# Chunked softmax attention on one core: where the softmax sum is divided out, and what runs ahead of the norm statistics

## The chip, the cores and the metric

One core of a Trainium2 chip runs the whole program in one launch. The metric is device time in microseconds (us), lower is better. The kernel before takes 3090.66 us, the median of three runs (3089.91 to 3095.58). Engines are named as in the profile: PE is TensorE (matrix products), PEld its weight loads, DVE is VectorE, ACT is ScalarE, POOL is GpSimd, SP is SyncE, which here only issues DMAs.

## The reference

A trunk of two layers over 1024 positions of width 1024, all in float32. Layer 0 holds two recurrent head groups, layer 1 the attention that is changed here; each layer ends in an MLP and a gated embedding. The attention, cut to what matters:

```python
def chunk_band_attention(h, w_qkv, q_g, k_g, rel_bias):       # h = rmsnorm(x, norm_mix_g[1])
    qkv = (h @ w_qkv).reshape(bsz, seq, 3, C_HEADS, C_HEAD_DIM)      # 16 heads of 64
    q = rmsnorm(qkv[:, :, 0], q_g) * (C_HEAD_DIM ** -0.5)
    k = rmsnorm(qkv[:, :, 1], k_g)
    v = qkv[:, :, 2]
    ...
    def one_chunk(c):                                         # 64 queries, 576 keys
        s = jnp.einsum('bqhd,bkhd->bhqk', q_c, k_b).astype(jnp.float32) + bias
        s = jnp.where(valid, s, -jnp.inf)
        prob = jax.nn.softmax(s, -1).astype(v.dtype)
        return jnp.einsum('bhqk,bkhd->bqhd', prob, v_b)
```

The softmax is exp(s - max) divided by its sum over the keys. The division can be done on the exponentials (a row of them has one query) or on the result of the product with v.

## The kernel before

**Numbers.** A float32 product is made from three products of a split type: each operand is rounded to float32r (hi) on ACT, and DVE computes the rest (lo). Hi times hi, hi times lo and lo times hi are added in PSUM. So each activation that is split costs one ACT and one DVE instruction (split_scaled, L349 to L353).

**The stages.** Layer 0 runs until about 880 us, its MLP and gate (tail) until 1680 us, the attention of layer 1 from there to about 2320 us, and then its tail. PE is given one order of work for the whole program.

**Order.** `run` drives several generators ("lanes") against a clock of its own (`self.now`, moved on by each matmul): a lane that yields the name of a stretch in the table LAT comes back when that many microseconds have gone by on this clock, and another lane is let in meanwhile. So LAT sets how much other PE work is placed between two stretches of one lane, and `attn_block1` is the time between a block's exponentials and its transposes. Beyond that, the order on each engine's queue is fixed when the program is built: instructions are placed when their operands are expected, earlier code first. On the chip each queue runs in this order; an instruction that waits holds up what stands behind it.

**Attention.** There are 16 steps (8 pairs of heads pr, times two halves hf of 512 queries). Four lanes run (layer1_in):

- `attn_ins` runs `attn_in` for each step: for 128 positions at a time (index i = 4 hf + e) 24 matmuls of 128x384 (q, k and v of a pair) into one PSUM bank (L1854 to L1856). The input is not yet divided by its root mean square. This factor belongs to a position, so it is applied when the bank is read: an ACT copy for q and k (L1861), an ACT copy (L1865) and a DVE rest (L1866) for v, all with `rscol[:, i]`. At the first projection of all, `row_stats` computes `rscol`: a matmul for each 128 positions of the squares (accs, added up by POOL at L1627, in two halves) with a column of ones, 16 in the trace, one DVE scaling (L375), and an inverse root in ten small DVE steps (rsqrt_small). The projections and the statistics take their banks from a pool of two (`self.bank`, profile name dps).
- `attn_norms` brings q and k to feature rows and splits them (F and Ql).
- Two lanes of `attn_block` share the 64 blocks (step, head h, block blk of 256 queries). A block has two query tiles m of 128. For each: scores of the near keys (bank sn) and the far keys (bank sf), bias and maximum on DVE (L1957, L1965, L1966), exponentials with their sum on ACT (L1967 far, L1970 near), sum (L1972), reciprocal (L1973), and a scaling of up to 640 exponentials by it on ACT (L1974). After `attn_block1`: transposes on PE into banks pt (L192), split into ptile (L349, L350), product with v into the bank po, whose rows are features and whose columns are queries. Behind the second block of a head, ACT copies one half of po (otmp, L2015), and DVE adds the other half to it, giving y (L2016, 64 rows of a head by 512 queries). After both heads y is stored by an SP DMA (L2022); the last y is split in place.

PSUM has eight banks here: two dps, two sn, one sf, one o (po), two pt. On the SP queue of the stage are weight loads (L1823, three of 512 KB for a pair, through two buffers wraw; splits L1824 and L1825), bias tables (toep, L1841) and stores of y.

Of the kernel before, what the change touches and what calls it, by code (L numbers as in the profile page):

```python
# [8 lines left out]
F32 = mybir.dt.float32  # L9
F32R = mybir.dt.float32r  # L10
I32 = mybir.dt.int32
AF = mybir.ActivationFunctionType
ALU = mybir.AluOpType
# [4 lines left out]
P = 128  # L18
T = 1024
D = 1024  # L20
NK = D // P
HB = 512
# [61 lines left out]
    "gdn_back4": 1.83,  # L84
    "attn_norm0": 0.24,
    "attn_block0": 0.97,
    "attn_block1": 4.45,
    "attn_block2": 0.43,
    "attn_block3": 0.94,
    "qk": 11.25,  # L90
# [19 lines left out]
class Trunk:  # L110
# [252 lines left out]
            nc.scalar.activation(sq, src, AF.Square)  # L363
            nc.gpsimd.tensor_tensor(acc, acc, sq, op=ALU.add)

    def row_stats(self, accs, out, scale=1.0 / D, eps=1e-6):

        nc = self.nc
        nt = out.shape[-1]
        ps = self.stat_bank()  # L370
        for i in range(nt):
            self.mm(ps[:, i:i + 1], accs[i // 4][:, (i % 4) * P:(i % 4 + 1) * P], self.ones[:, 0:1],
                             start=True, stop=True)
        ms = self.sm.tile([P, NT], F32, tag="ms", name="ms")[:, 0:nt]
        nc.vector.tensor_scalar(ms, ps[:, 0:nt], scale, eps, op0=ALU.mult, op1=ALU.add)  # L375
        self.rsqrt_small(out, ms, [P, nt], "n")
# [1451 lines left out]
    def attn_in(self, pr, hf, l1, kv):  # L1828

        nc, a, psm = self.nc, self.a, self.psm  # L1830
        V, A, G = nc.vector, nc.scalar, nc.gpsimd
        wp = self.wp
        if hf == 0:
            raw = lambda: self.wr.tile([P, T], F32, tag="wraw", name="wraw")
            w = self.load_qkv(pr, raw) if pr else self.wq
            kv.clear()
            kv.update(w=w, toep=[], vs=[])
            for h in range(2):
                hd = 2 * pr + h
                t = l1.tile([P, 3 * P], F32, tag="toep", name="toep", bufs=3)  # L1840
                nc.sync.dma_start(out=t, in_=a["rb"][hd])  # L1841
                kv["toep"].append(t)
        wh, wl = kv["w"]
        qk = wp.tile([P, 4, 256], F32, tag="qk", name="qk")
        vs = l1.tile([P, 4, 2, P], F32R, tag="vs", name="vs", bufs=4)
        kv["vs"] = kv["vs"] + [vs]
        for e in range(4):
            i = 4 * hf + e
            ps = self.bank([P, 3, P])
            ts = slice(i * P, i * P + P)  # L1850
            for k in range(NK):
                ks = slice(k * P, k * P + P)
                xh, xl = self.xg[k][:, 0, ts], self.xg[k][:, 1, ts]
                self.mm(ps, xh, wh[:, :, ks], start=k == 0, stop=False)  # L1854
                self.mm(ps, xh, wl[:, :, ks], start=False, stop=False)
                self.mm(ps, xl, wh[:, :, ks], start=False, stop=k == NK - 1)  # L1856
                yield 0
            if pr == 0 and i == 0:
                self.row_stats(self.accs, self.rscol)
            rc = self.rscol[:, i:i + 1]  # L1860
            A.activation(qk[:, e, :], ps[:, 0:2, :].rearrange("p a c -> p (a c)"), AF.Copy, scale=rc)  # L1861
            v3 = ps[:, 2, :].rearrange("p (h d) -> p h d", h=2)
            vf = vs[:, e].rearrange("p h c -> p (h c)").rearrange("p (q d) -> p q d", d=64)
            hi = vf[:, 0:4:3, :]
            A.activation(hi, v3, AF.Copy, scale=rc)  # L1865
            V.scalar_tensor_tensor(vf[:, 1:3, :], v3, rc, hi.bitcast(F32), op0=ALU.mult, op1=ALU.subtract)  # L1866
            yield 0
        q4 = qk.rearrange("p i c -> p (i c)").rearrange("p (n d) -> p n d", d=64)
        ss = self.sm.tile([P, 16], F32, tag="ss1", name="ss1")
        nn = self.sm.tile([P, 16], F32, tag="nn1", name="nn1")  # L1870
        for e in range(2):
            sq = wp.tile([P, 8, 64], F32, tag="sq", name="sq", bufs=1)
            G.tensor_tensor(sq, q4[:, 8 * e:8 * e + 8], q4[:, 8 * e:8 * e + 8], op=ALU.mult)
            V.tensor_reduce(ss[:, 8 * e:8 * e + 8], sq, op=ALU.add, axis=AX.X)
        V.tensor_scalar(ss, ss, 1.0 / 64, 1e-6, op0=ALU.mult, op1=ALU.add)
        self.rsqrt_small(nn, ss, [P, 16], "q")
        V.tensor_tensor(q4, q4, nn.rearrange("p (n o) -> p n o", o=1).broadcast_to((P, 16, 64)), op=ALU.mult)
        return dict(kv, qk=qk)
# [28 lines left out]
    def attn_block(self, s, pr, hf, h, blk, l1, rbl):  # L1907

        nc, psm, sm = self.nc, self.psm, self.sm
        V, A, G = nc.vector, nc.scalar, nc.gpsimd  # L1910
        st = self.st[s]
        m0 = 4 * hf + 2 * blk
# [4 lines left out]
        hs = slice(64 * h, 64 * h + 64)  # L1917
        Q, Ql, K, vs, toep = st["Q"], st["Ql"], st["K"], st["vs"], st["toep"][h]

        def score(ps, m, j0, n):  # L1920
            qs = slice((m % 4) * P, (m % 4) * P + P)
            o = 0
            while o < n:
                j = j0 + o
                e = min(n - o, 4 - j % 4)
                ks = slice((j % 4) * P, (j % 4 + e) * P)
                k = K[j // 4]
                self.mm(ps[:, o * P:(o + e) * P], Q[:, h, qs], k[:, h, ks], start=True, stop=False)
                self.mm(ps[:, o * P:(o + e) * P], Ql[h][:, qs], k[:, h, ks], start=False, stop=True)
                o += e  # L1930
# [6 lines left out]
        place, bank, off = {}, 0, 0  # L1937
        for j, c0, c1 in segs:
            if off + c1 - c0 > HB:
                bank, off = bank + 1, 0  # L1940
# [3 lines left out]
        for j, (b, o, c0, c1) in place.items():  # L1944
            used[b] = max(used[b], o + c1 - c0)
        probs = []
        for m in (m0, m0 + 1):
            n0 = max(0, m - 2)
            nn = m - n0 + 1
            f0 = max(0, m - 4)  # L1950
            nf = n0 - f0
            pn = psm.tile([P, HB], F32, tag="sn", name="sn", bufs=2)
            score(pn[:, 0:nn * P], m, n0, nn)
            mx = sm.tile([P, 4], F32, tag="mx", name="mx", bufs=4)
            pb = self.wp.tile([P, 5 * P], F32, tag="pb", name="pb", bufs=4)
            S = pb[:, nf * P:(nf + nn) * P]
            V.tensor_tensor_reduce(S, pn[:, 0:nn * P], toep[:, (3 - nn) * P:], op0=ALU.add, op1=ALU.max,  # L1957
                                   scale=1.0, scalar=NEG, accum_out=mx[:, 0:1])
            l = sm.tile([P, 4], F32, tag="l", name="l", bufs=4)
            if nf:  # L1960
                pf = psm.tile([P, HB], F32, tag="sf", name="sf")
                score(pf[:, 0:nf * P], m, f0, nf)
                if m >= 4:
                    V.memset(pf[64:128, 0:64], NEG)
                V.reduce_max(mx[:, 1:2], pf[:, 0:nf * P], axis=AX.X)  # L1965
                V.tensor_scalar(mx[:, 2:3], mx[:, 0:1], mx[:, 1:2], -1.0, op0=ALU.max, op1=ALU.mult)  # L1966
                A.activation(pb[:, 0:nf * P], pf[:, 0:nf * P], AF.Exp, bias=mx[:, 2:3], accum_out=l[:, 1:2])  # L1967
            else:
                V.tensor_scalar(mx[:, 2:3], mx[:, 0:1], -1.0, None, op0=ALU.mult)
            A.activation(S, S, AF.Exp, bias=mx[:, 2:3], accum_out=l[:, 0:1])  # L1970
            if nf:
                V.tensor_tensor(l[:, 0:1], l[:, 0:1], l[:, 1:2], op=ALU.add)  # L1972
            V.reciprocal(l[:, 2:3], l[:, 0:1])  # L1973
            A.activation(pb[:, 0:(nf + nn) * P], pb[:, 0:(nf + nn) * P], AF.Copy, scale=l[:, 2:3])  # L1974
            probs.append((pb, f0))
            yield "attn_block0"
        yield "attn_block1"

        job = 4 * s + 2 * h + blk
# [6 lines left out]
        for b in range(bank + 1):  # L1986
            pt = psm.tile([P, HB], F32, tag="pt", name="pt", bufs=2)
            for j, (bb, o, c0, c1) in place.items():
                if bb != b:
                    continue  # L1990
                for e in range(2):
                    if c0 <= 128 * e < c1:
                        pb, f0 = probs[e]
# [8 lines left out]
        q = 0  # L2002
        for j, c0, c1 in segs:
            b, o, _, _ = place[j]
# [4 lines left out]
        if blk == 1:  # L2009
            if h == 0:  # L2010
                st["y"] = l1.tile([P, HB], F32, tag="y", name="y", bufs=1)
            y, po = st["y"], st["po", h]
            oth = slice(64 * (1 - h), 64 * (1 - h) + 64)
            tmp = l1.tile([P, HB], F32, tag="otmp", name="otmp", bufs=1)
            A.copy(tmp[hs], po[oth])  # L2015
            V.tensor_tensor(y[hs], po[hs], tmp[hs], op=ALU.add)  # L2016
            if h == 1:
                if s == 15:
                    yield ("ylast", 0)
                    self.split_scaled(self.ylast, y, None, slice(0, HB))  # L2020
                else:
                    nc.sync.dma_start(out=self.yd[pr][hf], in_=y)  # L2022
                self.dump("y1", y, (pr, slice(None), slice(hf * HB, hf * HB + HB)))
                self.mark(("at", s))
# [92 lines left out]
```

## Time and profile before

| what | before |
|---|---|
| median of three runs | 3090.66 us |
| the profiled execution | 3089.73 us |
| its span in the trace | 3088.0 us |
| mean granted PE clock | 0.978 of full speed |
| ACT busy in the whole span | 1510.7 us (49%) |
| POOL busy in the whole span | 544.9 us (18%) |

How to read the rows: a group has line, engine, operation, output <- inputs by the program's names, shapes, count | busy us, mean ns | idle time of the engine just before them <- what ended it. A timeline row has the start in us from the beginning of the span, the length in us, then engine, line and operation, in brackets the idle time before it and its releaser. A wait row has who waited <- for whom: us in total, times, longest. A window row has start:end, length, then the busy time of PE, PEld, DVE, ACT and POOL with their instruction counts, then the granted PE clock, the share of the DMA engines and GB/s. L177 and L192 are the helpers that issue every matmul and every transpose, so these go by the names of their tiles.

### The profile page before, as it was taken

Reading aid. Unit: us, or ns where it says so; the run is one execution under the profiler, and the core shown is the slowest. Engines: PE = TensorE matmul, PEld = TensorE weight load, DVE = VectorE, ACT = ScalarE, POOL = GpSimd, SP = SyncE. Lnnn points to the kernel's source line nnn. Section 1 sums busy time; section 2 is a strip of 40 time slices with the busy share of each in tenths; the row PEclk is TensorE's granted clock in tenths of the full one; section 3 lists DMA queues with packets and bytes.
Section 4 is the critical chain, followed back from the end, with each engine's and each line's share of the span. In section 5 each row is a group of like instructions: output and inputs, shape, how many; then the busy total and the mean of one; then the engine's idle time right before and its main releaser. Section 6 shows DMA issues by size and latency. Waiting matters only on the chain.

```text
span 3088.0 us, 47130 instructions
## 1 busy us (share of the span) xinstructions
PE 2979.5 (96%) x17288; PEld 2461.2 (80%) x17288; DVE 2232.1 (72%) x4518; ACT 1510.7 (49%) x2922; POOL 544.9 (18%) x978
## 2 busy tenths in 40 slices
PE   7999999999999999999999999989899999999999
PEld 5777778777777888888887988888788888888887
DVE  6656676657849788878867666766768888888762
ACT  4333443334427544444434577777756544544431
POOL 6533442443500000000015111100110000000002
PEclk9999999999999999999999999999999999999999
DMA  4211112211346434754424101100256444754432
GB/s 138 72 54 62 55 55 74 62 53 64 125 158 219 158 148 150 259 167 150 137 89 144 34 33 36 53 33 16 72 177 225 151 154 150 255 172 150 126 109 102
DMA packets 187639, 358.45 MB, mean 116 GB/s; under 512 B 45712, under 2 KB 47888, under 8 KB 187408
## 3 DMA queue, kind: packets, MB, share of 16 engines
q1 hardware_dynamic: 158608, 303.00, 29.6%
q10 hardware_dynamic: 28800, 52.44, 4.4%
q8 instruction: 136, 2.23, 0.3%
q14 instruction: 95, 0.78, 0.1%
HBM read 262.04 MB, written 93.32 MB: 115 GB/s over the span
## 4 chain that ended last, share of the span: by engine, by line
PE 79%; DVE 10%; ACT 4%; DMA 3%; POOL 2%; issue 2%; SPq 0%; DVEq 0%; POOLq 0%; ACTq 0%
PE dps L177 66%; PE ch L177 2%; PE pm L177 2%; PE iz L177 1%; PE po L177 1%; PE tp L177 1%; DVE ptile L350 1%; PE pt L192 1%; DVE pb L1957 1%; PE sn L177 1%; POOL subt L415 1%; PE py L177 1%; DMA wraw<-in_w_qkv 1%; ACT pb L1970 1%; POOL sub L417 1%
## 5 line engine op out<-in xcount | busy, mean ns | idle before, releaser
L177 PE MATMUL dps<-r,act 128*128 128x512 f32 x3528 | 829.4, 392 | 0.0
L177 PEld LDWEIGHTS dps<-r,act 128*128 128x128 f32 x3528 | 662.0, 188 | 145.8
L177 PE MATMUL dps<-xg,whi 128*128 128x512 f32 x1280 | 434.0, 419 | 14.9 <-ACT xg L352 7.4
L1614 POOL TENSOR_TENSOR pn<-pn,prs 128x512 f32<-128x512 f32 x32 | 47.1, 1474 | 1543.1 <-ACT prs L386 1447.7
L177 PE MATMUL dps<-wq,act 128*128 128x384 f32 x1536 | 305.7, 345 | 6.4 <-DVE vs L1866 3.1
L177 PEld LDWEIGHTS dps<-xg,whi 128*128 128x128 f32 x1280 | 233.9, 195 | 67.9 <-issue 8.0
L177 PEld LDWEIGHTS dps<-wq,act 128*128 128x128 f32 x1536 | 266.6, 191 | 10.5 <-DVE vs L1866 4.9
L177 PE MATMUL dps<-xg,wlo 128*128 128x512 f32 x640 | 258.8, 405 | 1.3 <-DVE wlo L304 1.3
L177 PE MATMUL dps<-late,act 128*128 128x512 f32 x960 | 229.2, 392 | 0.0
L177 PEld LDWEIGHTS dps<-late,act 128*128 128x128 f32 x960 | 180.3, 188 | 39.7
L1271 ACT CAST act<-act 128x512 fp32r<-128x512 f32 (+1 forms) x223 | 137.6, 649 | 131.6 <-PE dps L177 67.5
L1384 DVE TENSOR_TENSOR late<-late,dps 128x512 f32<-128x512 f32 x224 | 152.4, 684 | 52.2 <-PE dps L177 45.8
L1271 ACT CAST act<-late 128x512 fp32r<-128x512 f32 x210 | 124.2, 617 | 133.2 <-PE dps L177 90.4
L177 PE MATMUL dps<-act 128*128 128x512 f32 x672 | 165.0, 392 | 0.0
L1272 DVE TENSOR_TENSOR act<-act 128x512 fp32r<-128x512 f32 (+1 forms) x223 | 154.8, 721 | 6.0 <-ACT act L1271 5.8
L177 PEld LDWEIGHTS dps<-act 128*128 128x128 f32 x672 | 126.1, 188 | 28.7
L1272 DVE TENSOR_TENSOR act<-late,act 128x512 fp32r<-128x512 f32 x210 | 141.5, 688 | 8.9 <-ACT act L1271 7.0
L177 PEld LDWEIGHTS dps<-xg,wlo 128*128 128x128 f32 x640 | 124.4, 194 | 29.2 <-DVE wlo L304 1.8
L303 ACT CAST whi<-wraw 128x1024 fp32r<-128x1024 f32 x78 | 81.9, 1050 | 122.0 <-PE dps L177 82.4
L1522 DVE TENSOR_TENSOR xw<-xw,dps 128x512 f32<-128x512 f32 x174 | 118.0, 683 | 31.5 <-PE dps L177 31.5
L177 PE MATMUL dps<-xw,act 128*128 128x512 f32 x576 | 139.6, 392 | 0.0
L1389 ACT ACTIVATE late<-late 128x512 f32<-128x512 f32 x128 | 80.3, 630 | 119.4 <-DVE late L1384 113.5
(484 smaller groups left out, 5656.7 us busy)
## 6 DMA issues: line engine op xcount, KB each, us to landing
hb<-late ACTq DMA_DIRECT2D x168, 256.0 KB
act<-hb SPq DMA_DIRECT2D x138, 256.0 KB
late<-in_w SPq DMA_DIRECT2D x60, 512.0 KB
wraw<-in_w_in SPq DMA_DIRECT2D x56, 512.0 KB
act<-in_w SPq DMA_DIRECT2D x96, 256.0 KB
braw<-hb SPq DMA_DIRECT2D x72, 256.0 KB
wraw<-in_w_out SPq DMA_DIRECT2D x21, 512.0 KB
wraw<-in_w_qkv SPq DMA_DIRECT2D x21, 512.0 KB
```

What stands on the lines that cost most here:

```text
L177: return self.begin(self.nc.tensor.matmul(out, lhsT, rhs, start=start, stop=stop, skip_group_check=again))
L192: return self.begin(self.nc.tensor.transpose(out, in_, ident))
L303: nc.scalar.copy(hi, raw)
L350: nc.vector.tensor_tensor(dst[:, 1, sl], src, dst[:, 0, sl].bitcast(F32), op=ALU.subtract)
L415: E.tensor_tensor(o, X[:, 0:i, i:i + 1].broadcast_to((NP, i, n)), Bq[:, i:i + 1, i + 1:16].broadcast_to((NP, i, n)), op=ALU.mult)
L417: E.tensor_tensor(X[:, 0:i, i + 1:16], X[:, 0:i, i + 1:16], o, op=ALU.add)
L1271: A.copy(hi, s)
L1272: V.tensor_tensor(lo, s, hi.bitcast(F32), op=ALU.subtract)
L1384: V.tensor_tensor(r, t, u, op=ALU.add)
L1389: A.activation(t, t, AF.Relu)
L1522: V.tensor_tensor(x[n][:, hs[hf]], x[n][:, hs[hf]], ps, op=ALU.add)
L1614: G.tensor_tensor(pn, pn, prs[:, sl], op=ALU.mult)
```

## The change

Three things are edited.

1. **The projections of the first pair.** The first two (i = 0, 1) write to the score banks sn, which no block uses yet; the third takes a bank of the pool as before. Their three scalings are held back (`held`). The statistics are computed behind the third projection, in a bank pt, and then the three scalings are done. From the fourth on all is as before.
2. **The softmax sum.** The scaling of the exponentials is gone. The two reciprocals of a block are written to one tile rl (128 positions by 2). An SP DMA writes it to a row in DRAM (256 values of 4 bytes), one for each block. Behind the second block of a head a further SP DMA reads this row of 512 values back, to each of the 64 feature rows of the head (R). After the addition that gives y, DVE multiplies y by R.
3. **LAT.** `attn_block1` is 3.60 instead of 4.45.

```diff
-    "attn_block1": 4.45,
+    "attn_block1": 3.60,
...
-    def row_stats(self, accs, out, scale=1.0 / D, eps=1e-6):
+    def row_stats(self, accs, out, scale=1.0 / D, eps=1e-6, bank=None):
...
-        ps = self.stat_bank()
+        ps = bank if bank is not None else self.stat_bank()
...
+        def scale(i, e, ps):
+            rc = self.rscol[:, i:i + 1]
+            A.activation(qk[:, e, :], ps[:, 0:2, :].rearrange("p a c -> p (a c)"), AF.Copy, scale=rc)
+            v3 = ps[:, 2, :].rearrange("p (h d) -> p h d", h=2)
+            vf = vs[:, e].rearrange("p h c -> p (h c)").rearrange("p (q d) -> p q d", d=64)
+            hi = vf[:, 0:4:3, :]
+            A.activation(hi, v3, AF.Copy, scale=rc)
+            V.scalar_tensor_tensor(vf[:, 1:3, :], v3, rc, hi.bitcast(F32), op0=ALU.mult, op1=ALU.subtract)
+        held = []
         for e in range(4):
             i = 4 * hf + e
-            ps = self.bank([P, 3, P])
+            if pr == 0 and i < 2:
+                ps = psm.tile([P, HB], F32, tag="sn", name="dps", bufs=2)[:, 0:3 * P].rearrange("p (a c) -> p a c", a=3)
+            else:
+                ps = self.bank([P, 3, P])
...
-            if pr == 0 and i == 0:
-                self.row_stats(self.accs, self.rscol)
-            rc = self.rscol[:, i:i + 1]
...
+            held.append((i, e, ps))
+            if pr == 0 and i == 2:
+                self.row_stats(self.accs, self.rscol, bank=psm.tile([P, HB], F32, tag="pt", name="st", bufs=2))
+            if pr or i > 1:
+                for h in held:
+                    scale(*h)
+                held.clear()
...
+        rl = sm.tile([P, 2], F32, tag="rl", name="rl", bufs=4)
+        if blk == 0:
+            st["rd", h] = self.dr.tile([1, HB], F32, tag=f"rd{h}", name="rd", bufs=2)
+            if h == 0:
+                st["R"] = l1.tile([P, HB], F32, tag="R", name="R", bufs=2)
...
-            V.reciprocal(l[:, 2:3], l[:, 0:1])
-            A.activation(pb[:, 0:(nf + nn) * P], pb[:, 0:(nf + nn) * P], AF.Copy, scale=l[:, 2:3])
+            V.reciprocal(rl[:, m - m0:m - m0 + 1], l[:, 0:1])
...
+        rd = st["rd", h]
+        nc.sync.dma_start(out=rd[:, 256 * blk:256 * blk + 256].rearrange("o (e q) -> (o q) e", e=2), in_=rl)
+        if blk == 1:
+            nc.sync.dma_start(out=st["R"][hs], in_=rd.broadcast_to((64, HB)))
...
             V.tensor_tensor(y[hs], po[hs], tmp[hs], op=ALU.add)
+            V.tensor_tensor(y[hs], y[hs], st["R"][hs], op=ALU.mult)
```

More of the change, by code (lines that the diff above doesn't have):

```diff
@@ L1857, in attn_in @@
                 yield 0
-            if pr == 0 and i == 0:
-                self.row_stats(self.accs, self.rscol)
-            rc = self.rscol[:, i:i + 1]
[L1861 to L1866, printed above, removed]
+            held.append((i, e, ps))
[5 more added lines that the diff above has]
+                held.clear()
             yield 0
```

## The prediction

> **What bounds the kernel now.** I read the page first (busy shares), then the sums of the attention stage, then who TensorE waited for in it.
>
> ```profile
> span 3088.0 us, 47130 instructions
> PE 2979.5 (96%) x17288; PEld 2461.2 (80%) x17288; DVE 2232.1 (72%) x4518; ACT 1510.7 (49%) x2922; POOL 544.9 (18%) x978
> ...
> 1694.00:2320.00 626.00, 577.91 (x3517) 535.15 (x3518) 431.38 (x1361) 435.92 (x1011) 76.33 (x75) 0.97 0.17 59
> ...
> PE pt L192 <- ACT pb L1974: 8.4, 9, 1.8
> PE po L177 <- ACT ptile L349: 6.6, 14, 1.0
> PE po L177 <- DVE ptile L350: 6.1, 11, 1.4
> PE dps L177 <- POOL acc L1627: 4.8, 2, 4.1
> PE sf L177 <- ACT pb L1967: 4.0, 7, 1.5
> PE pt L192 <- DVE ptile L350: 4.0, 9, 0.9
> PE dps L177 <- DVE vs L1866: 3.1, 7, 0.8
> ```
>
> TensorE is busy 96% of the span, and the change touches none of its matmuls. Only its idle time can be won. In the attention stage (third row: window, length, then busy time of PE, weight loads, DVE, ACT, POOL, then granted clock) that is 626.00 - 577.91 = 48.1 us; nothing before 1680 us and after 2320 us is edited. The wait rows (total, times, longest) divide most of it: 8.4 us for the normalised exponentials (L1974), 6.6 and 4.0 us for other ScalarE results, 13.2 us for VectorE, and 4.8 us, before the window begins, for the squares of GpSimd. VectorE and ScalarE are both about 69% busy there, so work taken from one and given to the other is not free.
>
> **Part 1: three projections ahead of the statistics.** The rows below are PE, then ACT, then DVE in order of time, and last 2 us slices with the granted clock as third number from the end.
>
> ```profile
> 1685.81 0.45 PE L177 MATMUL dps<-wq,act 128*128 128x384 f32 x1 [0.32 <-DVE act L353]
> 1686.93 1.05 PE L177 MATMUL dps<-ones,acc 128*128 128x1 f32 x8 [0.68 <-POOL acc L1627]
> 1692.09 1.86 PE L177 MATMUL dps<-ones,acc 128*128 128x1 f32 x8 [4.11 <-POOL acc L1627]
> 1694.60 8.72 PE L177 MATMUL dps<-wq,act 128*128 128x384 f32 x33 [0.64 <-DVE ms L375]
> ...
> 1701.79 0.47 ACT L1861 ACTIVATE qk<-dps,rscol 128x256 f32<-128x256 f32 x1 [3.52 <-PE dps L177]
> 1705.95 0.47 ACT L1861 ACTIVATE qk<-dps,rscol 128x256 f32<-128x256 f32 x1 [3.42 <-PE dps L177]
> 1710.11 0.47 ACT L1861 ACTIVATE qk<-dps,rscol 128x256 f32<-128x256 f32 x1 [3.42 <-PE dps L177]
> ...
> 1702.16 0.36 ACT L1865 ACTIVATE vs<-dps,rscol 128x128 fp32r<-128x128 f32 x1
> 1702.56 0.35 DVE L1866 SCALAR_TENSOR_TENSOR vs<-dps,rscol,vs 128x128 fp32r<-128x128 f32 x1 [3.40 <-ACT vs L1865]
> ...
> 1694.38 0.16 DVE L375 TENSOR_SCALAR ms<-dps 128x8 f32<-128x8 f32 x1
> 1696.59 0.17 DVE L291 SCALAR_TENSOR_TENSOR rscol<-rsw,rscol 128x8 f32<-128x8 f32 x1
> ...
> 1688.00:1690.00 2.00, 0.00 (x0) 0.00 (x0) 0.91 (x2) 1.24 (x2) 1.79 (x2) 1.00 0.97 378
> 1692.00:1694.00 2.00, 1.86 (x8) 1.78 (x8) 1.88 (x2) 1.05 (x1) 1.35 (x5) 0.50 0.08 31
> 1698.00:1700.00 2.00, 2.00 (x8) 2.00 (x7) 1.16 (x2) 0.28 (x2) 0.00 (x0) 0.50 0.07 16
> 1700.00:1702.00 2.00, 2.00 (x12) 2.00 (x11) 0.00 (x0) 0.21 (x1) 0.00 (x0) 0.86 0.67 246
> ```
>
> Now the first projection ends at 1686.26, the statistics wait for the second half of the squares until 1692.09, and the second projection starts at 1694.60. In the idle time the granted clock falls to 0.50, so that projection takes 1701.79 - 1694.60 = 7.2 us, where the next ones take 4.16 (distance of the ACT rows). The fourth ends at 1710.1.
>
> Changed: projections two and three run on at once, 1686.3 + 2 x 4.16 = 1694.6. The squares are there at 1692.1, so the 16 statistics products (8 in 1.05 us at full clock) end at 1696.7 and the fourth projection at 1700.9: 9.2 us earlier. The fifth then needs the bank of the third. rscol is ready 2.4 us after the products (DVE rows), at 1699.1, and three held pairs of scalings at 0.83 each (0.47 and 0.36) end at 1701.6; with 0.35 for the DVE part (L1866) the bank is free near 1702, a stall of 1.2. Net **-8.0 us**. The queues of POOL and SP hold nothing of what is moved. Bounds: -9.2 without the stall, -4.8 if only the wait for the squares goes, 0 if the stage takes it back (a rival). I take -8.0 because the pieces are measured at this place, and TensorE has no wait there that hangs on something else.
>
> The Trainium skill (TensorE: Matmul & The Clock Gate, Part 1) puts the way back to full clock at one busy window of about 3.4 us. Here it took from 1692.09 to beyond 1700, longer. By the page the second projection would have lost about 1.7 us instead of 3.0, and the gain would be 6.7; the measured slices decide, so 8.0 stays.
>
> **Part 2: no scaling of the exponentials.**
>
> ```profile
> 1802.00 1.50 ACT L1974 ACTIVATE pb<-pb,l 128x640 f32<-128x640 f32 x3
> ...
> L1974 ACT ACTIVATE pb<-pb,l 128x640 f32<-128x640 f32 (+4 forms) x128 | 86.2, 694 | 18.4 <-DVE l L1973 15.5 <-DVE ss L1875 1.6 <-DVE rsw L290 0.9
> L2016 DVE TENSOR_TENSOR y<-po,otmp 64x512 f32<-64x512 f32 x32 | 22.0, 687 | 6.2 <-ACT otmp L2015 5.8
> ```
>
> 128 activations go, 86.2 us of ACT's 435.9, a fifth. The 9 waits of the transposes for them total 8.4, so 0.93 each; one activation takes 0.69 and a row of three (first line) holds the transposes 1.5 us after the last exponential. Taking away 0.69 of each 0.93 wins 9 x 0.69 = 6.2: **-6.2** (0 to -8.4). The other ACT waits (6.6 + 4.0) arise in the same queue; a fifth less load makes them a fifth smaller: **-2.1** (0 to -10.6). What is late next is the split on VectorE.
>
> attn_block1 falls from 4.45 to 3.60: the transposes are placed 0.85 us earlier in TensorE's order, about what the activation took (0.69). So I count it zero; if the exponentials aren't earlier by that much, each of the 9 waits keeps its length and the -6.2 is gone.
>
> **Part 3: the multiplication.** 32 tensor_tensor of 64x512 are added on VectorE. The addition of that shape (L2016) reads PSUM and takes 0.687; from SBUF I take the same: 22.0 us. Most of it falls in VectorE's 195 us of idle time. The stretch below (chain of waits, start, length) shows where it doesn't.
>
> ```profile
> 1857.83 1.15 DVE wq L1825
> ...
> 1859.00 3.73 DMA wraw<-in_w_qkv
> 1862.75 1.06 ACT wq L1824
> ...
> 1866.74 0.68 DVE y L2016
> ...
> 1859.00 6.42 SPq L1823 DMA_DIRECT2D wraw<-in_w_qkv  x3
> ...
> ACT wq L1824 <- DMA wraw<-in_w_qkv: 7.1, 5, 3.4
> ```
>
> At such a pair boundary, where the next weights are loaded and split, the addition lies on the chain, and the multiplication would too. Seven boundaries x 0.69 = **+4.8** (0 to 22.0, all 32).
>
> **Part 4: the way through DRAM.** No row before moves 4-byte runs. The nearest is a write and read back in layer 0, in timeline rows; under it the tightest pair of sum and use that I found, a second head of an odd half.
>
> ```profile
> 101.37 0.50 SPq L420 DMA_DIRECT2D z<-sub  x1
> 103.71 0.38 SPq L422 DMA_DIRECT2D Xp<-z  x1
> 106.08 0.40 ACT L442 ACTIVATE T<-Xp,half 128x128 f32<-128x128 f32 x1 [6.56 <-DMA Xp<-z]
> ...
> 1941.31 0.22 DVE L1973 RECIPROCAL l<-l 128x1 f32<-128x1 f32 x2
> 1948.93 0.69 DVE L2016 TENSOR_TENSOR y<-po,otmp 64x512 f32<-64x512 f32 x1
> ```
>
> Write to read is 2.34 us, read to use 2.37: 4.7 together. From the last reciprocal to the end of the addition there are 1949.62 - 1941.53 = 8.1 us, 7.4 without one scaling. So R is there, 2.7 us before it is wanted: 0, as an estimate with bounds 0 (hidden by transposes, splits and value products) and 13 (rival 4). In VectorE's queue the running maxima and splits stand behind a late multiplication, and TensorE behind these. On SP 64 writes and 32 reads are new, at the 0.38 to 0.50 of these rows 36 to 48 us of a stage of 626; what could stand behind them is the weight load at a boundary (rival 3). The last step's y is multiplied while TensorE has projection work: 0.
>
> **Sum:** -8.0 - 6.2 - 2.1 + 4.8 = -11.5 us. The profiled execution took 3089.73 (span 3088.0 and 1.73 around it); so 3078.2 for it, and its time is 0.93 below the median of 3090.66: forecast **3079**.
>
> **The rivals.**
> 1. Only the entry pays. For: the transposes are moved 0.85 earlier and wait as before. Against: ACT is relieved by a fifth. 3090.7 - 8.0 = 3082.7.
> 2. The relief pays in full: -8.0 - 8.4 - 10.6 and nothing for VectorE, 3090.7 - 27.0 = 3063.7. Against it: VectorE as busy as ACT.
> 3. Slower: R's read waits on SP for the landing of the write (2.34 us), once per head, and the third weight load of a pair stands behind it. The last row of part 3 shows ACT waiting for weights already (7.1 us in 5 times), so ACT and VectorE have no room there. Two heads per boundary, 2 x 2.34 x 6 weight loads within the stage = 28 us: 3079 + 28 = 3107. It decides against the change from 11.5 / 6 = 1.9 us a boundary on. Against: the new issues fill under a tenth of SP's time, so few need meet a weight load.
> 4. R late at VectorE: a weight load of 3.73 us ahead on the rings makes 4.7 into 8.4, 1.0 over the 7.4, at most at 8 second heads; with the queue behind each stalled by the same again, 8 x 1.6 = 13: 3092. The Trainium skill (DMA: Bandwidth & Descriptors, Latency and other measured facts) speaks for it, with HBM access rising to 2 us at high load; no run here shows that.
> 5. The change doesn't do what it says at the entry: the stage takes the 8.0 back at a later wait, 3090.7 - 3.5 = 3087.2.
>
> **How the numbers follow.** Forecast 0.46, rivals 0.13, 0.12, 0.15, 0.07, 0.07. 0.2% is about what a measurement here can tell from no change: 6.2 us, so the borders are 3084.5 and 3096.8. Faster: 0.44 of the forecast, 0.09 of rival 1, 0.12 = 0.65; within: 0.02 + 0.04 + 0.06 + 0.06 = 0.18; slower: 0.15 + 0.01 + 0.01 = 0.17. The forecast's own range is 3072 to 3084; with rival 2 whole and most of 4, 5 and part of 3 it becomes 3063 to 3100.
>
> **What would show it.** Right: three projections without a gap and a granted clock of 1.0 from 1686 to 1700; no ACT group of 86 us; TensorE idle in the attention stage down from 48 to about 44 us, and y's multiplication without a wait for R. Wrong: VectorE waiting for R or ACT longer for weights (rivals 3, 4), transposes that wait for L1970 as they did for L1974 (rival 1), or steps that keep their old distance from 2200 us although the first came 8 us earlier (rival 5).

## The result, and the profile after

The changed kernel takes 3191.51 us, the median of five runs (3189.26 to 3196.59), beside 3089.91 for the kernel before on the same chip: a ratio of 1.0329, 95% interval 1.0313 to 1.0344. It is slower by 3.3%, outside the prediction's range of 3063 to 3100. The profiled execution took 3196.59 us.

First the page of the changed kernel, and its attention stage in one window (columns as in the prediction's window rows):

```profile
span 3194.9 us, 47306 instructions
...
PE 3007.7 (94%) x17288; PEld 2491.6 (78%) x17288; DVE 2252.2 (70%) x4550; ACT 1430.2 (45%) x2794; POOL 541.4 (17%) x978
...
1696.00:2425.00 729.00, 596.78 (x3476) 553.92 (x3476) 454.64 (x1392) 354.50 (x882) 77.41 (x76) 0.90 0.26 56
```

The stage is 729 - 626 = 103 us longer, which is nearly all of the 106.9 us in the span. TensorE's idle time in it went from 48.1 to 132.2 us; its busy time rose by 18.9 us, with 41 products fewer in the window, while the mean granted clock fell from 0.97 to 0.90. The work moved as intended: ACT is busy for 354.5 us in place of 435.9, and the transposes wait 3.4 us for its exponentials where they waited 8.4 us for the scaling. What is new stands in the wait rows, SP's first:

```profile
SPq L1994 <- DMA rd<-rl: 254.8, 32, 10.3
...
DVE y L2035 <- DMA R<-rd: 52.3, 15, 8.6
DVE y L2034 <- DMA yd<-y: 46.0, 5, 12.2
PE po L177 <- DVE y L2034: 40.9, 7, 12.4
ACT wq L1777 <- DMA wraw<-in_w_out: 33.5, 8, 7.8
ACT wq L1824 <- DMA wraw<-in_w_qkv: 20.2, 8, 4.9
```

Line 1994 is the read of R. It waits on SP for the write `rd<-rl` to land, 254.8 / 32 = 8.0 us each time, where the prediction had 2.34. VectorE waits for R, and longer each time (5 waits, 46.0 us) for a transfer that the change doesn't touch: the store of y (`yd<-y`), which must have read y before y is written again. Weight loads are late too (L1777: 12.5 us before). One such place in the chain of waits (start, length, what), and TensorE in its last stretch:

```profile
1819.43 0.22 DVE rl L1988 x2
1819.80 0.48 DVE ptile L350
1820.28 8.14 DMA rd<-rl
1828.48 0.45 SPq L1994
1829.03 0.54 SPq L1992
1829.62 9.90 DMA yd<-y
1839.61 0.69 DVE y L2034
1840.35 2.08 PE po L177 x8
...
1829.60:1839.50 9.90, 0.00 (x0) 0.00 (x0) 0.00 (x0) 0.60 (x2) 0.00 (x0) 0.50 0.21 40
```

A write of 1 KB is issued at 1820.28, and SP sits 8.14 us until it has landed. Only then can the finished y be stored, behind the next write (L1992). That store takes 9.90 us, and VectorE and TensorE stand still meanwhile; the granted clock falls to 0.50. The engines of the DMA aren't full: their mean share is 0.21 there.

The entry, in timeline rows of PE, then DVE, then ACT:

```profile
1686.62 9.11 PE L177 MATMUL dps<-wq,act 128*128 128x384 f32 x51 [0.86 <-ACT act L352]
1695.56 1.84 PE L177 MATMUL st<-ones,acc 128*128 128x1 f32 x16
1697.27 4.41 PE L177 MATMUL dps<-wq,act 128*128 128x384 f32 x24
1705.42 6.86 PE L177 MATMUL dps<-wq,act 128*128 128x384 f32 x29 [3.75 <-DVE vs L1854]
...
1699.61 1.23 DVE L1825 TENSOR_TENSOR wq<-wraw,wq 128x1024 fp32r<-128x1024 f32 x1 [3.10 <-ACT wq L1824]
1700.75 0.16 DVE L375 TENSOR_SCALAR ms<-st 128x8 f32<-128x8 f32 x1
...
1698.52 1.05 ACT L1824 CAST wq<-wraw 128x1024 fp32r<-128x1024 f32 x1 [3.27 <-DMA wraw<-in_w_qkv]
```

Three projections run on without a gap, as predicted, and the fourth ends at 1701.7. But the fifth waits 3.75 us in place of 1.2: the statistics were ready at 1697.4, and `ms` (L375) stood behind the split of a weight (L1825) in VectorE's queue, which waited for ACT, and ACT for the load.

### The profile page after: what moved, and what is told of

Read it like the earlier page. It is cut to its first block, busy times and chain, and to the rows that moved or that the text cites. A ratio compares the mean times of both kernels' runs of the same rounds, so it can differ in the third digit from the quotient of the medians.

```text
span 3194.9 us, 47306 instructions
## 1 busy us (share of the span) xinstructions
PE 3007.7 (94%) x17288; PEld 2491.6 (78%) x17288; DVE 2252.2 (70%) x4550; ACT 1430.2 (45%) x2794; POOL 541.4 (17%) x978
## 4 chain that ended last, share of the span: by engine, by line
PE 73%; DMA 11%; DVE 8%; ACT 3%; POOL 2%; issue 2%; SPq 0%; DVEq 0%; POOLq 0%; ACTq 0%
PE dps L177 62%; DMA rd<-rl 4%; PE ch L177 2%; DMA yd<-y 1%; PE pm L177 1%; PE iz L177 1%; DMA wraw<-in_w_out 1%; PE po L177 1%; DMA R<-rd 1%; PE tp L177 1%; DMA wraw<-in_w_qkv 1%; POOL sub L417 1%; PE py L177 1%; PE sn L177 1%; POOL subt L415 1%
## 5 line engine op out<-in xcount | busy, mean ns | idle before, releaser
L177 PE MATMUL dps<-wq,act 128*128 128x384 f32 x1536 | 315.7, 355 | 10.4 <-DVE vs L1854 5.8
L177 PEld LDWEIGHTS dps<-wq,act 128*128 128x128 f32 x1536 | 278.6, 199 | 13.9 <-DVE vs L1854 6.9
L177 PE MATMUL po<-ptile,vs 128*128 128x256 f32 (+1 forms) x576 | 114.7, 313 | 63.7 <-DVE y L2034 40.9
L177 PEld LDWEIGHTS po<-ptile,vs 128*128 128x128 f32 x576 | 93.6, 215 | 72.7 <-DVE y L2034 31.6
```

The lines of the kernel that those rows point to most:

```text
L177: return self.begin(self.nc.tensor.matmul(out, lhsT, rhs, start=start, stop=stop, skip_group_check=again))
```

## The experiments

Four readings were open: the write's landing is long and all DMAs behind it come late; SP's wait blocks what stands behind it in its queue; R alone is late at VectorE; y's one buffer is the trouble. The table has the runs of the whole kernel; each ratio is to runs of the kernel before on the same chip. The last column is from one profile each: the span less the start of the first product of the attention with v, so that the entry is left out. It must be read with care where the entry itself differs: a shorter entry makes the first product earlier, and what the stage then takes back counts against that version.

| kernel | median us | ratio to before, 95% interval | first product to end, us |
|---|---|---|---|
| before | 3089.91 | 1 | 1341.4 |
| changed | 3191.51 | 1.0329 (1.0313 to 1.0344) | 1452.8 |
| e1 part 1 alone | 3086.54 | 0.998 (0.9968 to 0.9992) | 1336.9 |
| e2 no DMA | 3073.88 | 0.9934 (0.9916 to 0.9952) | 1324.1 |
| e3 DMAs, none awaited by VectorE | 3188.62 | 1.0298 (1.0275 to 1.0321) | 1446.0 |
| e4 runs of 8 bytes | 3091.17 | 0.9989 (0.9977 to 1.0) | 1341.4 |
| e5 two buffers for y | 3184.35 | 1.0289 (1.0263 to 1.0316) | 1428.9 |
| e6 = e4, reads from GpSimd | 3089.08 | 0.9982 (0.997 to 0.9995) | 1344.6 |
| e7 4 bytes, reads from GpSimd | 3207.99 | 1.0366 (1.0347 to 1.0384) | 1457.3 |
| e8 part 1 alone, four banks | 3081.02 | 0.9958 (0.9944 to 0.9972) | 1337.6 |
| e10 = e4, two y, four banks | 3083.57 | 0.9966 (0.9956 to 0.9976) | 1345.7 |
| e11 = e10, reads from GpSimd | 3088.89 | 0.9981 (0.9969 to 0.9994) | 1350.2 |
| e12 runs of 16 bytes | 3081.37 | 0.9967 (0.9957 to 0.9977) | 1329.5 |
| e13 = e12, four banks | 3084.75 | 0.9979 (0.9967 to 0.999) | 1344.1 |
| e14 = e13, two y | 3080.87 | 0.9967 (0.9958 to 0.9976) | 1341.8 |

**Which part costs.** e1 keeps the entry and puts the scaling of the exponentials back; e2 keeps all but the DMAs, and so leaves out the division.

```diff
-            V.reciprocal(rl[:, m - m0:m - m0 + 1], l[:, 0:1])
+            V.reciprocal(l[:, 2:3], l[:, 0:1])
+            A.activation(pb[:, 0:(nf + nn) * P], pb[:, 0:(nf + nn) * P], AF.Copy, scale=l[:, 2:3])   # e1
...
-        nc.sync.dma_start(out=rd[:, 256 * blk:256 * blk + 256].rearrange("o (e q) -> (o q) e", e=2), in_=rl)
-        if blk == 1:
-            nc.sync.dma_start(out=st["R"][hs], in_=rd.broadcast_to((64, HB)))                        # e1, e2
...
-            V.tensor_tensor(y[hs], y[hs], st["R"][hs], op=ALU.mult)
+            V.tensor_tensor(y[hs], y[hs], self.R1[hs], op=ALU.mult)      # e2, e3: a constant row
```

> Three projections ahead of the statistics, the exponentials scaled as before, attn_block1 at 4.45: part 1 alone. Before: 3090. Theory A (the loss is all in the way through DRAM): the fifth projection starts 4.6 us earlier relative to the end of the layer before, as in the changed kernel (1705.42 - 1.74 = 1703.7 against a fourth projection that ended at 1710.1 and a fifth that ended at 1714.3 before), and the stage keeps it: 3085 to 3086. Theory B (the stage takes it back at a later wait): 3089 to 3091. Theory C (part 1 shares in the loss): above 3095.

> The changed kernel without its 96 DMAs: y is multiplied by a constant tile, so the division by the softmax sum is left out. Theory A (the DMAs are the whole loss): what is left is part 1, the relieved ACT and the added multiplication, about -4.6 - 8.3 + 4.8 against before: 3078 to 3086. Theory C (the multiplication, attn_block1 or another order lose too): above 3095, and above 3150 if they are the larger part.

The entry alone gains 0.2%, 6 us. Without the 96 DMAs the changed kernel is 0.66% faster than before; so they cost 1.0329 - 0.9934 = 0.0395, 122 us. Against e1 the relief of ACT, with the multiplication and the shorter attn_block1 (which wasn't tried by itself), gains 0.0046 of 3090, 14 us; by the two intervals that is 7 to 21. In e2 this row is all that the transposes wait for ACT, in place of 8.4 us:

```profile
PE pt L192 <- ACT pb L1983: 1.0, 4, 0.3
```

**Who has to wait.** e3 issues all the DMAs, but multiplies y by the constant, so that VectorE doesn't wait for R (the division is left out here too). e5 gives y two buffers, e7 moves the reads of R to GpSimd's queue, so that SP doesn't wait for a landing.

```diff
-                st["y"] = l1.tile([P, HB], F32, tag="y", name="y", bufs=1)
+                st["y"] = l1.tile([P, HB], F32, tag="y", name="y", bufs=2)       # e5
...
-            nc.sync.dma_start(out=st["R"][hs], in_=rd.broadcast_to((64, HB)))
+            G.dma_start(out=st["R"][hs], in_=rd.broadcast_to((64, HB)))          # e7
```

> The changed kernel with all its DMAs, but y is multiplied by a constant tile, so nobody waits for R and the division is left out. Theory A1 (R late at VectorE is the loss, 52.3 us of waits in the profile): most of it goes, 3080 to 3110. Theory A2 (SP stands still for the landing of each write, and the store of y and the weight loads come late): VectorE still waits for the store of y and SP for the landing, 3140 to 3185.

> The changed kernel with two buffers for y, so the addition of the next head pair need not wait for the store of the last one. Theory S (SP stands still behind the landing of each write, the store of y goes out late, and VectorE and TensorE wait for the one y): the 46.0 us of VectorE's waits for the store go; SP still stands still for 250 us and weight loads stay late: 3130 to 3160. Theory W (weight loads and tables behind SP are the larger part): 3170 to 3190.

> The changed kernel (runs of 4 bytes), with only the 32 reads of R issued by GpSimd's queue. The writes stay on SP, but nothing on SP waits for a landing any more. Theory S: SP's 255 us of waits for the landing go, R is late by the rest of the landing: 3085 to 3125. Theory Q (a write of 4-byte runs holds back what is behind it on the rings, the store of y and the weights, whoever waits for it): 3150 to 3190.

None of the three brings back more than 0.4%; e3 and e7 came out slower than any of their theories had it. Wait rows of e3, where R is read and not used (lines are two further on):

```profile
DVE y L2036 <- DMA yd<-y: 67.1, 5, 17.6
PE po L177 <- DVE y L2036: 63.1, 7, 15.5
```

The wait for R (52.3 us) is gone, and that for the store of y has grown from 46.0 to 67.1. With two buffers (e5) it is the other way round: the store is no longer waited for, and the waits for R grow to 81.3 us. In e7 the chain of waits and the wait rows say why SP's queue isn't the cause:

```profile
1819.65 9.66 DMA rd<-rl
...
1829.38 9.98 DMA R<-rd
...
1819.18 8.32 SPq L1992 DMA_DIRECT2D rd<-rl  x4
...
POOL R L1994 <- DMA rd<-rl: 359.3, 30, 39.4
DVE y L2035 <- DMA R<-rd: 74.2, 14, 12.3
```

The read of R is on GpSimd's queue, and its own write (9.66 us) has landed when it is issued; still it lands only 9.98 us later. Meanwhile SP had issued further writes (third row: four from 1819.18 on, the last at 1827.1, 2.2 us ahead of the read). So each remedy for one waiter hands the wait to the next: the DMAs themselves come late.

**What makes them late.** e4 puts the two reciprocals of a position side by side in DRAM: the same 1 KB and the same number of DMAs, but 128 runs of 8 bytes in place of 256 of 4. R comes in another order, which the multiplication undoes. e6 is e4 with the reads on GpSimd's queue.

```diff
-        nc.sync.dma_start(out=rd[:, 256 * blk:256 * blk + 256].rearrange("o (e q) -> (o q) e", e=2), in_=rl)
+        nc.sync.dma_start(out=rd[:, 256 * blk:256 * blk + 256].rearrange("o (q e) -> (o q) e", e=2), in_=rl)
```

> The two reciprocals of a position lie side by side in the DRAM row, so a write has 128 runs of 8 bytes in place of 256 of 4; R is read with the two tiles interleaved. Theory R (the landing of 8.1 us goes with the number of runs): it falls to 4.5 to 5.5 us, and the time to 3100 to 3140. Theory F (the landing is a fixed time of small or late writes): it stays at 8 us and the time at 3180 to 3195.

> Runs of 8 bytes, and the 32 reads of R are issued by GpSimd's queue, so that SP waits for no landing. The kernel with runs of 8 bytes and reads on SP took 3091.2, the one without DMAs 3073.9. Theory S (what is left of the loss is SP's 93 us of waits for landings): 3074 to 3082. Theory B (what is left is R late at VectorE, or the rings shared with the loads): 3087 to 3095. GpSimd's own work behind a wait could add to either.

```profile
SPq L1994 <- DMA rd<-rl: 93.3, 32, 5.5
```

The landing falls from 8.0 to 93.3 / 32 = 2.9 us, further than either theory had it, and with it go 0.034 of the time, 105 us of the 122. What is left, 17 us against e2, doesn't go with the queue either (e6 and e4 overlap).

**The writes by themselves.** m1 puts loads of 512 KB alone and behind small writes; its eight kinds of write were issued mixed with one another and tell little, so m2 repeats them one after the other, VectorE waiting for each.

```diff
+    case("r4x256near", 2, 256, lambda d: d.rearrange("o (e q) -> (o q) e", e=2))
+    case("r4x128far", 1, 2048, lambda d: d.rearrange("o (q w) -> (o q) w", w=16)[:, 0:1])
...
+    by4 = lambda e, d: e.dma_start(out=d.rearrange("o (e q) -> (o q) e", e=2), in_=small)
+    by8 = lambda e, d: e.dma_start(out=d.rearrange("o (q e) -> (o q) e", e=2), in_=small)
```

> Leaves out the whole computation (x alone is copied to the output), so its time is not compared. Eight kinds of write, four times each, each followed by a one-element read-back that waits for the write to land; then a 512 KB load alone, behind an 8-byte write, behind a 4-byte write on the same queue and behind a 4-byte write issued on ACT's queue. Theory (4-byte runs that share a line are what lands late): the two writes of neighbouring 4-byte runs (256 and 128 of them) land in 5 to 10 us, the more runs the later, all writes of 8 bytes or more within 3 us, also with 256 runs; the load behind a 4-byte write is ready 5 us or more later than the load alone, behind an 8-byte write less than 1 us later. Rival A (the number of runs): all three kinds with 256 runs take 5 us or more, all with 128 about 2.5. Rival B (4 bytes whatever lies beside): the 4-byte runs 64 bytes apart are as late as the neighbouring ones. Rival C (it takes the load of the attention stage beside it): all land within 3 us here.

> Leaves out the whole computation (x alone is copied to the output), so its time is not compared. Eight kinds of write to DRAM, four of each, one after the other: VectorE rewrites the source between them and so waits for each write to land. Theory (what is slow is 4-byte runs that lie beside one another, which share a stretch of memory and are written piece by piece): 256 neighbouring runs of 4 bytes take about 8 us, 128 of them about 4 to 5, 4-byte runs 64 bytes apart and all runs of 8, 16 and 64 bytes 2 to 3.5 us, 256 of them too. Rival A (the number of runs): all kinds with 256 runs take about 8 us, all with 128 about half. Rival B (a run of 4 bytes costs more wherever it lies): the 4-byte runs 64 bytes apart are as late as the neighbouring ones, 256 runs of 8 bytes stay below 3.5 us.

The chain of waits of m1 (a write with runs of 8 bytes, two of the loads that were issued behind such a write, then a write with runs of 4 bytes and three loads behind such a write; `wafter` is the load):

```profile
81.30 3.38 DMA after<-small
...
85.66 5.96 DMA wafter<-in_x
...
92.37 6.97 DMA wafter<-in_x
...
106.52 7.96 DMA after<-small
...
115.55 11.64 DMA wafter<-in_x
...
127.99 13.01 DMA wafter<-in_x
...
141.74 13.03 DMA wafter<-in_x
...
0.73 3.29 DMA x<-in_x
...
136.00:139.00 3.00, 0.00 (x0) 0.00 (x0) 1.00 0.37 20
139.00:141.00 2.00, 0.00 (x0) 0.00 (x0) 1.00 0.31 123
```

A load behind an 8-byte write is there after 6 to 7 us, behind a 4-byte write after 11.6 to 13.0. The loads issued with no write ahead are no good measure, since stores of 512 KB ran beside them (4 to 6 us); but a load of the same size ahead of all writes (x, third row from the end) took 3.29 us. So a load behind a small write takes about its own time and that write's landing (3.0 and 8 us) together, and the expected delay of less than 1 us behind 8 bytes was too short. The small write holds up a transfer 500 times its size. Whether a write on ACT's queue does so too stays open here: in those four cases the copy was released by the write itself, 8.5 to 12.2 us after its issue. The Trainium skill (DMA: Bandwidth & Descriptors, Queues, rings and completion order) has a rule that bears on it: the step that raises a DMA's semaphore lands only after every earlier write of the same DMA engine, across its queues. Nothing here contradicts it, and e7's read on another queue fits. But the rule is about the completion alone, and in m1 the load itself is late: in the last two rows (start:end, length, busy times of VectorE and GpSimd, clock, DMA share, GB/s) its bytes still move at 20 GB/s 8 to 11 us after its issue at 127.99, and nearly half of them come in the last 2 us. What holds them up isn't shown.

The wait rows of m2, four writes of each kind (name: bytes of a run, number of runs; near: one run beside the next, far: 64 bytes apart):

```profile
DVE sw L2093 <- DMA r4x256near<-sw: 35.0, 4, 10.4
DVE sw L2093 <- DMA r4x128near<-sw: 29.9, 4, 7.8
DVE sw L2093 <- DMA r8x256near<-sw: 14.5, 4, 4.2
DVE sw L2093 <- DMA r8x128near<-sw: 12.2, 4, 3.1
DVE sw L2093 <- DMA r64x256near<-sw: 7.5, 4, 2.5
DVE sw L2093 <- DMA r4x256far<-sw: 6.7, 4, 1.7
DVE sw L2093 <- DMA r16x128near<-sw: 6.1, 4, 1.5
DVE sw L2093 <- DMA r4x128far<-sw: 6.0, 4, 1.5
```

Neighbouring runs of 4 bytes wait 8.8 us on average, of 8 bytes 3.0 to 3.6, of 16 bytes 1.5. Half the runs change little (7.5 for 128), so the number isn't it; and 4-byte runs that lie 64 bytes apart land in 1.5 to 1.7, so the 4 bytes alone aren't either. That short runs share a stretch of memory which is written piece by piece fits all eight rows, but no row shows the inside of the memory, or what the DMA engines do to one another there. In m2 the writes go one at a time, between the first load and the last stores: the landing needs no load beside it.

**Taking the landing away.** e12 keeps the way through DRAM, but writes once for each head, four reciprocals of a position side by side. e10, e11, e13 and e14 add a second y, four banks at the entry, or both (e8 has the four banks with part 1 alone).

```diff
-        nc.sync.dma_start(out=rd[:, 256 * blk:256 * blk + 256].rearrange("o (e q) -> (o q) e", e=2), in_=rl)
         if blk == 1:
+            nc.sync.dma_start(out=rd.rearrange("o (q m) -> (o q) m", m=4), in_=st["rl", h])          # e12
...
-            if pr == 0 and i < 2:
-                ps = psm.tile([P, HB], F32, tag="sn", name="dps", bufs=2)[:, 0:3 * P].rearrange("p (a c) -> p a c", a=3)
+            if pr == 0 and i < 4:
+                tag = ("sn", "sn", "sf", "o")[i]
+                ps = psm.tile([P, HB], F32, tag=tag, name="dps", bufs=2 if i < 2 else 1)[:, 0:3 * P].rearrange("p (a c) -> p a c", a=3)   # four banks
```

> Part 1 alone, with the first four projections in banks of the attention (two sn, sf, o), so the fifth and sixth find both banks of the pool free. Part 1 with two such banks took 3086.5, and TensorE waited 3.75 us ahead of the fifth projection. Theory A: that wait goes: 3082 to 3084. Theory B (the stage takes it back at its first blocks): 3086 to 3088.

> The changed kernel with runs of 8 bytes, a second buffer for y and the first four projections of an entry in four banks. If the 17 us that the 8-byte version still lies above the version without the DMAs are the wait of y for its store and the entry's third bank, both gone here: 3070 to 3080, below the four banks alone (3081). If they are completions that come late behind the writes, whoever waits: 3081 to 3090, and not below the four banks alone.

> The same with the reads of R issued by GpSimd, so that SP waits for no write to land. If SP's waits behind the 8-byte writes (93 us in all, 1 to 3 us each) still delay weight loads: 5 us or more below the version with the reads on SP. If what is left hangs on landings and not on the queue that waits: within 3 us of it.

> The changed kernel with one write of 128 runs of 16 bytes for each head in place of two of 256 runs of 4 bytes. If the landing is the whole loss: SP waits 1 to 2 us for each write (32 writes, 30 to 60 us in all), VectorE not for y's store, and the time is that of the version without the DMAs within 5 us: 3074 to 3080. If the extra DMAs and SP's waits cost something of their own: as with 8-byte runs, 3086 to 3091.

> The same with the entry's first four projections in four banks. With the landing short the entry's gain (5.5 us, from part 1 alone 3086.5 to four banks alone 3081) comes on top: 3068 to 3076. If the way through DRAM disturbs the entry or eats the gain: 3076 to 3082, no better than the four banks alone.

> The same with a second buffer for y. If y's store is no longer waited for, within 2 us of the version with one buffer; if it is still late now and then, 3 to 6 us below it.

SP's wait in e12, and the row of the value products in the changed kernel and in e12 (shortest/median/longest in ns, start of the first and of the last):

```profile
SPq L1994 <- DMA rd<-rl: 48.3, 32, 3.0
```

```profile
L177 PE MATMUL po<-ptile,vs x576: 218/282/584, 1742.1 to 2412.0; 128*128 128x256 f32 x144, 128*128 128x128 f32 x48
```

```profile
span 3085.5 us, 47233 instructions
...
L177 PE MATMUL po<-ptile,vs x576: 219/280/454, 1756.0 to 2303.3; 128*128 128x256 f32 x144, 128*128 128x128 f32 x48
```

The same row of e13:

```profile
L177 PE MATMUL po<-ptile,vs x576: 219/280/581, 1745.0 to 2304.2; 128*128 128x256 f32 x144, 128*128 128x128 f32 x48
```

In e12, 48.3 / 32 = 1.5 us a landing, as m2 has it for 16 bytes. From first to last product it is 547.3 us where the changed kernel has 669.9. The time is 0.9967 of before: a third of a per cent faster with the same algorithm that was 3.3% slower. Of the 0.0395 that the DMAs cost, 0.0362 go with the short landing (and half of the write DMAs, which alone can't be that much: e4 kept them all). The rest, 0.0033 or 10 us by the ratios and 5 us by the last column, is what else e12 has and e2 hasn't. One piece of it is seen in the groups of e12:

```profile
L2036 DVE TENSOR_TENSOR y<-y,R 64x512 f32<-64x512 f32 x32 | 34.8, 1086 | 0.7
```

Reading R in steps of 16 bytes, the multiplication takes 1.086 us in place of 0.693, 32 x 0.393 = 12.6 us on VectorE; how much of that is on the path wasn't tried. In e4, in steps of 8 bytes, it takes 0.692.

The four banks take the entry's stall away (in e8 projections, statistics and projections follow on one another without a gap up to 1715 us), and e8's ratio is 0.0022 below that of e1, 7 us, though their intervals overlap. With e12 it was expected to add up, to 3068 to 3076, and didn't: e13 and e14 stand at 0.9979 and 0.9967, since from the first product on they need 12 to 15 us more than e12. Nine of these are the entry's own gain: from the first projection to the first product e12 takes 62.5 us, e13 53.5 and e14 53.8. The stage takes them back, and 4 to 6 us more: from the first projection to the end it is 1392.0, 1397.6 and 1395.6 us, in one profile each. At which wait it does so stays open. For the same reason e10 and e11, which have the four banks too, say little about what is left of the loss with runs of 8 bytes; they bring e4 no further than the four banks alone. So four versions that compute the whole are at 0.9958 to 0.9967, and their intervals overlap; e8, the smallest edit, has the lowest ratio.

## Why the prediction was wrong

- **Part 4, the way through DRAM at 0: this step failed.** It took the landing of the write from the row `z<-sub`, 2.34 us, as the nearest; measured it is 8.0 in the kernel and 8.8 alone. Those runs were of 2 KB, and m2 shows that the length of neighbouring runs decides: 8.8, 3.0 and 1.5 us for 4, 8 and 16 bytes. The part itself said that no row before moves 4-byte runs, but set the upper bound (13 us) with the same 2.34. Its second gap: it looked for what is queued behind the waiting read on SP, and not for DMAs that land late behind the write wherever they are issued. These cost 122 us, with the store of y and TensorE's clock among them.
- **Rival 3** had the right sign and place (SP's read waits for the landing), but priced it at 2.34 and at weight loads alone, 28 us. e7 takes its mechanism away, SP's wait, and is not faster: the wait on the queue by itself is not what costs.
- **Rival 4** (R late at VectorE, 13 us) is seen, 52.3 us in 15 waits. e3 takes that wait away and is at 1.0298: the y store is late in its place. The rival's own sum is off as well: 1.0 us, stalled by the same again, is 2.0, so 8 x 2.0 = 16 and not 13.
- **Part 1, -8.0.** e1 gains 0.2% with an interval of 2.5 to 9.9 us, so it is not contradicted, but the rows name the difference: no gap and a clock of 1.0 as forecast, and a stall of 3.75 us in place of 1.2. The prediction followed rscol from the products on, and left out that `ms` has a weight split ahead of it in VectorE's queue, which hangs on a load.
- **Parts 2 and 3, -8.3 + 4.8 = -3.5.** The multiplications are 32 of 0.693 us, as predicted. But e2 against e1 has 14 us (7 to 21): the transposes' waits for ACT fall from 8.4 to 1.0 us, more than the 6.2 of the sum. The relief was under-sized, and the measured value is nearer to rival 2 (19.0) than to the sum; how the 14 us divide between relief, multiplication and attn_block1 wasn't tried.
- **The sum.** With short landings the sum is about right: e12, the change with another layout in DRAM, has 0.9967 x 3090.66 = 3080.5 where 3079 was forecast. That it comes so near is in part luck: without the DMAs the gain is 20 us (e2) and not 11.5, and e12 gives about 10 of it back, in part perhaps by its slower multiplication. So one term was wrong, by some 120 us, and the others were off by up to 10 us in both directions.

## What to carry to other kernels

When small values go through DRAM, look at how many bytes lie together at the destination, not at how many there are in all: side by side in runs of 16 bytes they landed five times sooner than in runs of 4, with half the writes, at the price of a permuted read. A late write must be priced with what is issued after it, on another queue too (e7); if one waiter after the other is relieved and the wait only moves, the transfer itself is the cause. Where no row shows a transfer of the kind that a change adds, a bound that rests on the nearest row of another kind is no bound: a write measured by itself settles it.

## What the runs showed of the hardware

- The landing of a small write to DRAM depends on the length of neighbouring runs (m2): 8.8 us for 4 bytes, 3.0 for 8, 1.5 for 16, and 1.5 to 1.7 again for 4-byte runs 64 bytes apart. The Trainium skill (DMA: Bandwidth & Descriptors, Specifications) puts a read-modify-write below 512 bytes; by these rows that alone doesn't make a write slow.
- A load of 512 KB issued behind a write of 256 runs of 4 bytes lands 5 to 7 us later than behind one of 128 runs of 8 bytes (m1), though both move 1 KB. Either way it takes about as long as the write's landing and the load ahead of all writes (3.29 us) together.
- VectorE's multiplication of 64x512 takes 0.693 us with all operands in order, 0.692 with one read in steps of 8 bytes (e4), and 1.086 in steps of 16 (e12). The Trainium skill (SBUF — State Buffer, Door 1) has 16-byte lines there that need two hits each for full bandwidth; the three figures agree.
- TensorE's granted clock was 0.50 in a standstill of 9.9 us, and 0.90 over the stage (0.97 before). The 103 us by which the stage got longer are 84 us of further idle time and 19 us of longer busy time.
